# Second half of the DeltaNet's q ahead of the LRU's gate, and four square roots in one activation

## The chip, the cores and the metric

The kernel runs on one core of a Trainium2 chip. The metric is device microseconds (us) for one execution. A core has five engines with an instruction stream each: TensorE (PE, matmuls; PEld is its weight load), VectorE (DVE), ScalarE (ACT), GpSimd (POOL) and SyncE (SP, which issues most DMAs). Each engine works through its stream in the order that was written when the kernel was built, and waits on semaphores for the others.

## The reference

One layer of a hybrid diffusion backbone, for 512 latent tokens and 128 context tokens with the same weights. A normalised and modulated input goes through one wide projection `w_in`; its columns feed four mixers, each run forward and backward; their outputs go through `w_out`, then a SwiGLU feed-forward block, then a last norm. Two mixers matter here, cut to the steps that do:

```python
# RG-LRU (each direction): x = dwconv(u_x), gate = gelu(u_gate)
r, i = sigmoid(x @ w_r + b_r), sigmoid(x @ w_i + b_i)
a = exp(-8 * r * softplus(-lambda))
h = scan(a, sqrt(1 - a * a) * i * x)          # h_t = a_t h_{t-1} + b_t
out = (h_forward + h_backward) * gate

# gated DeltaNet (each direction, chunks of tokens)
q, k, v = split(silu(dwconv(u_qkv)))
A = strict_tril((k beta) k^T * decay)         # needs k
attn = tril(q k^T * decay)                    # needs q and k
u, w = solve(I + A, [v beta, k beta exp(g)])
```

## The kernel before, in words

**Staging.** Everything is fp32, with projections as three products of a high and a low part. The 640 tokens are five tiles of 128 (t = 0 to 3 latent, 4 context). The run has four parts: norms and the first projections (to about 65 us), the rest of the input projections with the mixers' first steps (65 to 350), the scans, Hyena's transforms and the output projection (350 to 580), and the feed-forward block (580 to the end).

**A projection** (`inproj`, line 490 for its load, 504 for its matmuls) makes 128 columns of `w_in` for all tokens. It loads 512 KB into one of four `raw` buffers on SP; ACT casts the high part (line 166, tile `h_g` for a DeltaNet column block, `h_lg` for a gate of the LRU, `h_s` for the SSD), DVE makes the low part (line 162); both go into two slots each (tags `hi` and `lo`). Then come 48 matmuls, 24 for each half of 320 tokens, each half in one of three PSUM banks (tag `ip`). `conv_` (lines 530 to 542) copies both halves from PSUM into one of two pads (`xpad`, lines 534 to 536), multiplies by the first tap on ACT (539) and adds the other taps on DVE (542); `conv_silu` adds a tanh on ACT (526) and a product on DVE (527).

**The DeltaNet.** `g_q(0)` and `g_q(1)` project the two halves of q into `qT[0]` and `qT[1]`; g_q(1) is called at line 989. `EN(t)` (line 999) makes, for each tile and direction, the decay matrix (`gd`, matmuls at 738 and 739, exponential on ACT at 740 into one of three `Eh` buffers), the products k k^T and k q^T (`pkk`, lines 1013 and 1014, which read both halves of q), and on DVE (line 162) the products `Nm` and `Eh`; the latter is stored to `at_d` by a DMA of POOL (1019). One of the `Eh` buffers is later the place of `xsT[0]`, which `ssd_in(0)` writes. With all of `Nm` there, the inverse begins at line 1075: `A1` is cleared (1084) and filled by copies (1078 is their helper), transposed into `Lm` (1091, 1092), inverted in 15 steps on DVE, and merged to larger blocks (`g_merge`, lines 1135 to 1199, tiles `pg`, `pu`, `b0m`, `b1m`). `A1` and its neighbours take the memory that the LRU gives back at line 1059 (`la.close()`).

**The LRU.** For i = 0, 1 and both directions: `lru_m(i)` (line 909) has gate matmuls (917), tanh on ACT (918, 920) and a product on DVE (921). `lru_x2(i)`, named `lru_f0` and `lru_f1` in the list of priorities, has an exponential and a square on ACT (940, 941) and a product on DVE (942). `lru_q` takes the square root of that product (949), `lru_e(i)` multiplies, scans (960) and combines. `lru_g(i)` projects the gate, `lru_h(i)` makes its gelu.

**What sets the order.** No order is written out by hand. Each step names itself with `PR("name")`, which looks up a number in `PRI` (lines 36 and 37): among what is ready on an engine, a planner that simulates the time when the kernel is built takes the smaller number first. Loads of weights have 11144 taken off (`HPW`), convolutions 466 (`HPC`). Numbers that matter: `g_q0` 2384, `g_q1` 5036, `lru_g0` 2433, `lru_g1` 2240, `lru_m1` 2421, `lru_f0` 1412, `lru_f1` 3633, `lru_q` 2553, `lru_e0` 1709, `lru_e1` 2530, and for `EN` `g_N0` to `g_N4` (163 to 705) and `g_A0` to `g_A4` (334 to 2820).

**Tiles of the LRU.** Two tiles `ar0` and `ar1` of [128, 7, 642] hold seven slots each (lines 876, 877); `slot(i, 4)` and `slot(i, 5)` are the inputs and results of the square roots.

Of the kernel before, what the change touches and what calls it, by code (L numbers as in the profile page):

```python
# [10 lines left out]
F32 = mybir.dt.float32  # L11
F32R = mybir.dt.float32r
AF = mybir.ActivationFunctionType
# [5 lines left out]
P = 128  # L19
# [10 lines left out]
CW = 642  # L30
# [5 lines left out]
PRI = {'start': -944, 'mod00': 2696, 'hyk11': 1265, 'mod0b': 2465, 'ln1': 1628, 'mod01': 2955, 'ln1a': 167, 'mod02': -718, 'ln1b': 103, 'pcb': 223, 'ln1c': 1485, 'hyk10': 417, 'psj': 1862, 'zs0': 2044, 'zm0': -455, 'zs1': 881, 'zm1': 8, 'zs2': -414, 'zm2': 393, 'ze': 1399, 'dt': 933, 'g_k0': 2123, 'g_k1': 2629, 'g_kch': 972, 'lru_x0': 1527, 'hyk1b': 1451, 'lru_x1': 1575, 'hyk20': 544, 'hyk21': 1740, 'hyk22': 1814, 'hyk23': 1707, 'hyk24': 1990, 'g_kc2': 276, 'g_q0': 2384, 'lru_m': 2899, 'lru_k': 1498, 'g_q1': 5036, 'lru_m0': 406, 'lru_m1': 2421, 'g_0': 4095, 'g_N1': 163, 'g_A1': 1465, 'lru_g0': 2433, 'lru_f1': 3633, 'lru_g1': 2240, 'g_N3': 705, 'g_A3': 334, 'lru_f0': 1412, 'g_N2': 541, 'g_A2': 635, 'g_v0': 548, 'g_v1': 2397, 'g_N0': 172, 'g_A0': 2820, 'lru_h0': 2965, 'lru_h1': 2619, 'g_N4': 593, 'g_A4': 618, 'ssd_i0': 2774, 'lru_q': 2553, 'lru_e0': 1709, 'ssd_i1': 2822, 'lru_e1': 2530, 'g_vt': 1745, 'lru_s': 2094, 'g_nq': 2189, 'ssd_i3': 2918, 'ssd_i2': 2870, 'gz1': 3762, 'hy_v0': 1937, 'gz0': 2627, 'hy_10': 4373, 'mod20': 2831, 'g_base': -389, 'hy_v1': 2055, 'hy_11': 2440, 'mod21': 1302, 'g_mg': 2913, 'hy_00': 2567, 'mod22': 2350, 'hy_01': 2595, 'mod23': 1837, 'g_m4': 1148, 'g_m03': 1303, 'g_m12': 2034, 'g_scan': 3264, 'ssd_0': 3102, 'g_u40': 2369, 'g_u41': 2320, 'g_u00': 1882, 'g_u01': 2336, 'g_u30': 557, 'g_u31': 2358, 'g_u10': 2369, 'g_u11': 2380, 'g_u20': 1806, 'g_u21': 2402, 'g_s40': 4492, 'g_s41': 2958, 'mod40': 2376, 'ssd_p4': 5380, 'mod41': 2698, 'g_s00': 601, 'g_s31': 2981, 'ssd_p0': 3161, 'g_s10': 2343, 'g_s21': 2586, 'mod42': 2634, 'g_o4': 2441, 'g_f4': 2509, 'ssd_p3': 3197, 'mod30': 1471, 'ssd_p1': 3326, 'g_s20': 2566, 'g_s11': 3455, 'mod43': 307, 'g_o1': 2401, 'g_f1': 1956, 'g_s30': 2992, 'ssd_p2': 2893, 'g_s01': 3006, 'g_o3': -46, 'g_f3': 2760, 'mod31': 4255, 'ssd_e': 4063, 'g_o2': 2169, 'g_f2': 883, 'g_o0': 697, 'g_f0': 1847, 'po_lru': 2438, 'po_lru1': 2582, 'mod32': 2201, 'mod33': 1666, 'po_lru0': 1699, 'po_gdn': 5099, 'po_gdn1': 5500, 'mod50': 2718, 'po_gdn0': 4149, 'po_ssd': 3645, 'mod51': 556, 'po_ssd1': 4259, 'po_ssd0': 4824, 'hy_c': 4288, 'hy_t': 3649, 'hy_f4': 2554, 'mod52': 89, 'hy_f3': 2521, 'hy_f1': 2545, 'hy_f2': 2488, 'hy_f0': 2124, 'hy_y1': 664, 'hy_y0': 4124, 'gam': 412, 'po_x4': 1254, 'po_x1': 4228, 'po_x2': 4233, 'po_x0': 3441, 'po_x3': 3747, 'po_s': 2293, 'out04': 482, 'out01': 2542, 'out02': 9821, 'out00': 8067, 'out03': 6014, 'out14': 2981, 'out11': 4232, 'out12': 6019, 'out10': 3671, 'out13': 5720, 'ln2': 3582, 'mod53': -782, 'ffn': 2467}  # L36
PRI.update({'g_scan': 2100, 'g_u40': 2200, 'g_u41': 2220, 'g_u20': 2240, 'g_u21': 2260, 'g_u30': 2280, 'g_u31': 2300, 'g_u10': 2320, 'g_u11': 2340, 'g_u00': 2360, 'g_u01': 2380, 'g_s40': 2400, 'g_s41': 2420, 'g_s00': 2440, 'g_s31': 2460, 'g_s10': 2480, 'g_s21': 2500, 'g_s20': 2520, 'g_s11': 2540, 'g_s30': 2560, 'g_s01': 2580, 'hy_c': 1000, 'hy_t': 2600, 'g_o4': 2660, 'g_f4': 2720, 'hy_f0': 2780, 'hy_f1': 2840, 'hy_f2': 2900, 'g_o1': 2960, 'g_f1': 3020, 'hy_f3': 3080, 'g_o2': 3140, 'g_f2': 3200, 'hy_f4': 3260, 'hy_y0': 3320, 'g_o0': 3380, 'g_f0': 3440, 'hy_y1': 3500, 'g_o3': 3560, 'g_f3': 3620, 'mod40': 2700, 'mod41': 2850, 'mod42': 3000, 'mod43': 4200, 'gam': 3000, 'ln2': 4955, 'ffn': 6500, 'ln2b': 5080, 'ffn0': 5050, 'ssd_0': 3000, 'ssd_p4': 3700, 'po_lru': 2500, 'po_hy': 3690, 'po_lru0': 3720, 'ssd_p0': 3780, 'ssd_p1': 3830, 'ssd_p2': 3880, 'ssd_p3': 3930, 'po_lru1': 3980, 'ssd_e': 4040, 'ssd_m0': 4070, 'ssd_y0': 4100, 'po_hy0': 4130, 'po_gdn': 4190, 'ssd_m1': 4210, 'ssd_y1': 4240, 'po_hy1': 4270, 'mod30': 3780, 'po_gdn0': 4350, 'ssd_m2': 4410, 'ssd_y2': 4440, 'po_gdn1': 4470, 'ssd_f0': 4530, 'po_x0': 4540, 'out0': 4550, 'mod31': 3830, 'mod32': 4070, 'mod33': 4080, 'ssd_m3': 4610, 'ssd_y3': 4640, 'ssd_f1': 4670, 'po_x1': 4680, 'out1': 4690, 'h20': 4720, 'ssd_m4': 4740, 'ssd_y4': 4770, 'mod50': 4949, 'ssd_f2': 4820, 'po_x2': 4830, 'out2': 4840, 'h21': 4870, 'ssd_f3': 4900, 'po_x3': 4910, 'out3': 4920, 'h22': 4950, 'ssd_f4': 4970, 'po_x4': 4980, 'out4': 4990, 'h23': 5020, 'h24': 5040, 'mod51': 5019, 'mod53': 5039, 'po_ssd': 4000, 'po_s': 4000, 'po_w': 4470, 'ffn_w': 4845, 'ffn_s': 5080})
RG = {'pkv': 1, 'psz': 1, 'px': 1, 'pso': 1, 'pst': 1, 'p0': 1, 'sd': 1, 'pcb': 1, 'pce': 1, 'py': 1}
PRLOG = []

ROWS = {}
# [101 lines left out]
def body(nc, tc, I, O, dbg=()):  # L143
    ctx = ExitStack()
    with ctx:
        _body(ctx, nc, tc, I, O, dbg)


def _body(ctx, nc, tc, I, O, dbg):
    V, S, G, PE, SY = nc.vector, nc.scalar, nc.gpsimd, nc.tensor, nc.sync  # L150

    def PR(name):
        if name in PRI:
            tc.cur_priority = PRI[name]
        PRLOG.append((name, tc.cur_priority))

# [26 lines left out]
    def ring(k, dflt):  # L183
        return (psi, ps)[RG.get(k, dflt)]

# [687 lines left out]
    lp = la.enter_context(tc.tile_pool(name="lp", bufs=1, side="right"))  # L873


    ar = [lp.tile([P, 7, CW], F32, name=f"ar{i}") for i in range(2)]
    slot = lambda i, k: ar[i][:, k]
    bd = [pool.tile([P, 2, 2, P], F32, tag=tg, name=f"bd{tg}") for pool, tg in ((qkp, "kT1"), (mixp, "xsT1"))]
    PR("lru_m")
    for gi, nm in enumerate(("lru_w_r", "lru_w_i")):  # L880
# [62 lines left out]

    def lru_q():
        PR("lru_q")
        for i in range(2):
            for d in range(2):
                u = slot(i, 4 + d)
                S.activation(u, u, AF.Sqrt, scale=0.25)

    def lru_e(i):
        PR(f"lru_e{i}")
# [75 lines left out]
    g_v(1)  # L1028
    EN(1)
    lru_q()  # L1030
    lru_e(0)
    EN(0)
# [838 lines left out]
    for q in range(FT // 2):  # L1871
# [4 lines left out]
        u = acp.tile([P, NTOK], F32, tag="u", bufs=1, name=f"u{q}")  # L1876
# [140 lines left out]
```

## Time and profile before

| what | value |
|---|---|
| median of 3 runs | 1005.34 us (1001.15 to 1012.11) |
| the profiled execution's own time | 1005.17 us |
| its span, first to last instruction | 1003.4 us |
| mean granted clock of TensorE in the span | 0.965 |

The rows that follow the change are from the profiled execution. Times in them are microseconds from the start of the span, unless marked ns. A row of a timeline is: start, duration, engine, line, operation, what it writes and reads, how many instructions it merges, and in brackets the idle time ahead of it and what ended that. A row of instruction groups has busy time and mean duration in ns, then the idle time in front of the group. TensorE's clock has two levels, 1.2 and 2.4 GHz; the profile gives the mean granted share of the higher one.

### The profile page before, as it was taken

The numbers are of one execution on the slowest core, as the hardware profiler recorded it, in microseconds if no ns is written. First come the engines' busy times: TensorE is split into PE (matmuls) and PEld (weight loads), VectorE is DVE, ScalarE is ACT, GpSimd is POOL, SyncE is SP. The second block draws the span as 40 slices with busy tenths as digits, with TensorE's granted clock in tenths as the row PEclk, the third lists the DMA queues.
The fourth block names the chain that finished last, engine by engine and source line by source line (L and its number), as shares of the span: only waits on it lengthen the run. The fifth ranks groups of instructions, "written<-read, shape, count | busy, mean of one in ns | idle before, by whom it ended". The sixth has DMA issues, their size and how long they took to land.

```text
span 1003.4 us, 17283 instructions
## 1 busy us (share of the span) xinstructions
PE 949.8 (95%) x6837; PEld 820.8 (82%) x6837; DVE 649.5 (65%) x1162; ACT 443.2 (44%) x827; POOL 254.7 (25%) x262
## 2 busy tenths in 40 slices
PE   5999999999989999989998699999999999999995
PEld 2788887989868877866666599999999998888884
DVE  3667756869840257456799998777777777414115
ACT  3585287565565441134236454444444446122112
POOL 3115400221110120000354665444444420002001
PEclk9999996999987999999999799999999999999998
DMA  9983510432320654444234233222223336312202
GB/s 316 298 247 81 171 43 21 129 108 65 107 75 3 203 171 122 142 157 143 62 108 158 85 106 84 85 85 85 85 84 86 87 91 215 92 62 98 71 21 105
DMA packets 100654, 114.29 MB, mean 114 GB/s; under 512 B 13493, under 2 KB 77370, under 8 KB 100573
## 3 DMA queue, kind: packets, MB, share of 16 engines
q1 hardware_dynamic: 94748, 103.56, 33.7%
q0 software_dynamic: 5824, 9.63, 3.2%
q8 instruction: 54, 0.88, 0.4%
q14 instruction: 28, 0.22, 0.1%
HBM read 100.39 MB, written 12.24 MB: 112 GB/s over the span
## 4 chain that ended last, share of the span: by engine, by line
PE 78%; DVE 8%; ACT 6%; DMA 3%; issue 3%; POOL 2%; SPq 0%; POOLq 0%; ACTq 0%; DVEq 0%
PE dn L1959 15%; PE ip_g L504 4%; PE ip_h L504 3%; PE pm L358 3%; PE ip_s L504 2%; PE pplru L1581 2%; PE pphy L1581 1%; PE ip_hv L504 1%; PE pzz L589 1%; PE hpy L1398 1%; PE pab L1374 1%; PE pv L1234 1%; PE ip_gz L504 1%; PE ip_lg L504 1%; DVE x2a L162 1%
## 5 line engine op out<-in xcount | busy, mean ns | idle before, releaser
L1959 PE MATMUL dn<-h_d,alo 128*128 128x512 f32 x220 | 86.4, 393 | 0.2 <-DVE alo L162 0.2
L1959 PE MATMUL dn<-l_d,ahi 128*128 128x512 f32 x220 | 86.4, 397 | 0.0
L1959 PE MATMUL dn<-h_d,ahi 128*128 128x512 f32 x220 | 85.1, 393 | 0.6 <-DVE u L162 0.5
L162 DVE TENSOR_TENSOR l_d<-r_d,h_d 128x1024 fp32r<-128x1024 f32 x22 | 27.0, 1226 | 77.9 <-ACT h_d L166 76.6
L166 ACT CAST h_d<-r_d 128x1024 fp32r<-128x1024 f32 x22 | 23.1, 1048 | 93.9 <-PE dn L1959 82.7
L1959 PEld LDWEIGHTS dn<-h_d,alo 128*128 128x128 f32 x220 | 41.4, 188 | 10.6 <-DVE alo L162 0.5
L1959 PEld LDWEIGHTS dn<-h_d,ahi 128*128 128x128 f32 x220 | 41.2, 188 | 10.5 <-DVE u L162 0.9
L1959 PEld LDWEIGHTS dn<-l_d,ahi 128*128 128x128 f32 x220 | 41.3, 188 | 9.0
L358 PE MATMUL pm<-wm,sc 128*32 128x256 f32 (+1 forms) x320 | 33.8, 472 | 2.8 <-ACT sc L291 2.8
L1992 POOL TENSOR_TENSOR x<-x,aux 128x512 f32<-128x512 f32 x5 | 7.3, 1462 | 96.2 <-ACT aux L1989 96.2
L264 POOL TENSOR_TENSOR ss<-ss,mh 128x1 f32<-128x1 f32 (+1 forms) x11 | 8.0, 727 | 89.0 <-DVE ss L1945 71.7
L731 POOL DMA_DIRECT2D RT<-grd x20 | 11.1, 559 | 73.4 <-PE pce L1528 44.2
L1826 POOL TENSOR_TENSOR sms<-r_u,sms 128x512 f32<-128x512 f32 x11 | 14.9, 1352 | 45.7 <-DVE op_g4S L162 4.5
L264 POOL TENSOR_TENSOR ro<-ro,mh 128x4 f32<-128x4 f32 x5 | 5.4, 1089 | 74.2 <-DVE ro L267 74.2
L1826 POOL TENSOR_TENSOR sms<-r_g,sms 128x512 f32<-128x512 f32 x11 | 14.7, 1334 | 35.8 <-DVE op_u5S L162 4.3
L360 ACT COPY mr<-pm 128x256 f32<-128x256 f32 (+1 forms) x20 | 8.3, 413 | 29.9 <-PE pm L358 27.7
L162 DVE TENSOR_TENSOR l_h<-r_h,h_h 128x1024 fp32r<-128x1024 f32 x4 | 4.8, 1212 | 25.3 <-ACT h_h L166 17.9
L1822 POOL TENSOR_TENSOR sms<-sms,r_u 128x512 f32<-128x512 f32 x11 | 16.6, 1506 | 11.0 <-DVE op_g0S L162 4.7
L162 DVE TENSOR_TENSOR alo<-act,ahi 128x640 fp32r<-128x640 f32 x22 | 18.1, 824 | 1.4
L528 POOL MEMSET xpad<- 128x2 f32 x10 | 1.0, 100 | 69.8 <-DVE kT L527 22.9
L1820 POOL TENSOR_TENSOR sms<-r_u,r_u 128x512 f32<-128x512 f32 x11 | 14.4, 1311 | 16.7 <-DVE tmp L162 2.5
L358 PEld LDWEIGHTS pm<-wm,sc 128*32 128x32 f32 x320 | 9.8, 113 | 10.8 <-issue 3.8
(1294 smaller groups left out, 2949.0 us busy)
## 6 DMA issues: line engine op xcount, KB each, us to landing
wm<-w_mod SPq DMA_DIRECT2D x48, 512.0 KB, 4.9
r_g<-w_gate SPq DMA_DIRECT2D x22, 512.0 KB, 3.8
r_u<-w_up SPq DMA_DIRECT2D x22, 512.0 KB, 5.1
r_d<-w_down SPq DMA_DIRECT2D x22, 512.0 KB, 3.9
cs<-k_cs POOLq DMA_DIRECT2D x8, 512.0 KB, 6.0
r_g<-w_in SPq DMA_DIRECT2D x6, 512.0 KB, 6.6
xs_dram<-xt SPq DMA_DIRECT2D x5, 512.0 KB
at_d<-Eh POOLq DMA_DIRECT2D x10, 256.0 KB, 2.4
```

What stands on the lines that cost most here:

```text
L162: V.tensor_tensor(out, a, b, op=op)
L166: S.copy(hi, src)
L264: last_pow[0] = G.tensor_tensor(ap, ap, m.to_broadcast(list(ap.shape)), op=ALU.pow)
L358: last_mm[0] = PE.matmul(pm[j * 32:j * 32 + 32, :w], sc2[:, kt, :], wms[kt // nk][:, kt % nk, :], start=(kt < 4), stop=(kt >= 4))
L504: PE.matmul(pj[:, :320], a[:, kt, :], b[:, kt, c], start=(n == 0), stop=(n == 23))
L589: PE.matmul(pzz[t][:, :280], hx[:, k0 + k, t * P:(t + 1) * P], w[:, k, :], start=(q == 0 and n == 0), stop=(q == 2 and n == 3 * nk - 1))
L731: G.dma_start(RT[32 * d + 8:32 * d + 10, b], grd[m * 8 + d * 4:m * 8 + d * 4 + 4, :, t].rearrange("h a c -> a h c"))
L1581: PE.matmul(po, a[:, i, tk], b[:, i], start=(n == 0), stop=(n == last))
L1820: G.tensor_tensor(sf("S1"), A[1, 0], A[1, 1], op=ALU.add)
L1822: G.tensor_tensor(sf("S2"), sf("S1"), A[0, 0], op=ALU.subtract)
L1826: G.tensor_tensor(sf("S4"), A[0, 1], sf("S2"), op=ALU.subtract)
L1959: PE.matmul(po[t], a[f][:, tk], b[:, i, :], start=(f == 0 and pi == 0), stop=(f == FT - 1 and pi == 2))
```

## The change

The step `g_q1` gets the number 2390 in place of 5036, so it comes right behind `g_q0`. The two tiles of the LRU become one tile `ar` of five slots for each i and one tile `au` of the two slots that the square roots use; the slots' places change and their sum stays at 14. `lru_q` takes the square root of all of `au`, 2568 columns, with one activation in place of four of 642.

```diff
 RG = {'pkv': 1, 'psz': 1, 'px': 1, 'pso': 1, 'pst': 1, 'p0': 1, 'sd': 1, 'pcb': 1, 'pce': 1, 'py': 1}
+PRI.update({'g_q1': 2390})
 PRLOG = []
...
-    ar = [lp.tile([P, 7, CW], F32, name=f"ar{i}") for i in range(2)]
-    slot = lambda i, k: ar[i][:, k]
+    ar = lp.tile([P, 2, 5, CW], F32, name="ar")
+    au = lp.tile([P, 2, 2, CW], F32, name="au")
+    slot = lambda i, k: au[:, i, k - 4] if k in (4, 5) else ar[:, i, min(k, 4)]
...
     def lru_q():
         PR("lru_q")
-        for i in range(2):
-            for d in range(2):
-                u = slot(i, 4 + d)
-                S.activation(u, u, AF.Sqrt, scale=0.25)
+        S.activation(au, au, AF.Sqrt, scale=0.25)
```

## Rows read from the trace of the kernel before

**Rows 1.** The page: busy time of the engines, and granted clock in 40 slices.
```profile
PE 949.8 (95%) x6837; PEld 820.8 (82%) x6837; DVE 649.5 (65%) x1162; ACT 443.2 (44%) x827; POOL 254.7 (25%) x262
...
PEclk9999996999987999999999799999999999999998
```

**Rows 2.** PE by stretches: stretch, length, busy (instructions), granted clock, DMA share, GB/s.
```profile
140.00:180.00 40.00, 38.10 (x188) 0.79 0.15 40
180.00:230.00 50.00, 49.79 (x330) 1.00 0.31 99
230.00:240.00 10.00, 8.14 (x45) 0.83 0.20 59
240.00:280.00 40.00, 40.00 (x410) 1.00 0.41 118
280.00:330.00 50.00, 44.50 (x1029) 0.76 0.12 37
330.00:420.00 90.00, 89.89 (x804) 1.00 0.52 155
```

**Rows 3.** Waits of PE, 100 to 350: total us, times, longest.
```profile
PE pu L1198 <- ACT b1m L1194: 2.6, 1, 2.6
PE ip_s L504 <- ACT xpad L534: 2.1, 1, 2.1
PE gd L738 <- ACT ar L918: 1.9, 1, 1.9
```

**Rows 4.** Timeline of PE, 130 to 188.
```profile
131.20 1.58 PE L504 MATMUL ip_g<-hhi,h_g 128*128 128x320 f32 x8
...
150.33 0.90 PE L504 MATMUL ip_g<-hhi,h_g 128*128 128x320 f32 x5
153.12 0.49 PE L738 MATMUL gd<-RT,LT 10*128 10x512 f32 x1 [1.90 <-ACT ar L918]
...
159.45 2.33 PE L504 MATMUL ip_lg<-hhi,h_lg 128*128 128x320 f32 x8
...
173.71 1.34 PE L504 MATMUL ip_g<-hhi,l_g 128*128 128x320 f32 x8
...
187.44 0.71 PE L1014 MATMUL pkk<-qT,knT 64*128 64x128 f32 x8
```

**Rows 5.** Groups of ACT's instructions, 125 to 185.
```profile
L949 ACT ACT_TABLE_LOAD x4 | 5.1, 1283 | 0.1
...
L949 ACT ACTIVATE ar<-ar 128x642 f32<-128x642 f32 x4 | 3.0, 741 | 0.0
...
L166 ACT CAST h_lg<-r_lg 128x1024 fp32r<-128x1024 f32 x2 | 2.1, 1046 | 5.3 <-PE ip_g L504 5.3
...
L918 ACT ACT_TABLE_LOAD x1 | 1.3, 1283 | 0.0
```

**Rows 6.** Timeline of SP's queue: loads of q's weights.
```profile
63.92 2.55 SPq L490 DMA_DIRECT2D r_g<-w_in  x2
```

**Rows 7.** Groups of DVE's instructions, 185 to 225.
```profile
L162 DVE TENSOR_TENSOR Eh<-pkk,Eh 128x256 f32<-128x256 f32 x20 | 8.0, 419 | 0.1
L162 DVE TENSOR_TENSOR Nm<-pkk,Eh 128x256 f32<-128x256 f32 x20 | 7.9, 417 | 6.3 <-PE pkk L1014 5.5 <-ACT Eh L740 0.8
```

**Rows 8.** Groups of DVE's instructions, 125 to 185.
```profile
L960 DVE TENSOR_TENSOR_SCAN ar<-ar,colv 128x512 f32<-128x512 f32 x4 | 5.1, 1279 | 0.1
L162 DVE TENSOR_TENSOR ar<-ar 128x642 f32<-128x642 f32 x6 | 4.9, 825 | 10.4 <-ACT ar L949 10.4
...
L960 DVE TENSOR_TENSOR_SCAN ar<-ar 128x128 f32<-128x128 f32 x4 | 1.6, 399 | 0.0
```

**Rows 9.** The chain that ended last, 209 to 233: start, us, what.
```profile
214.78 2.76 DMA at_d<-Eh
...
225.51 2.11 DVE Lm L1092
```

**Rows 10.** Timeline of POOL: the clear of the inverse's first tile.
```profile
182.31 0.74 POOL L1084 MEMSET A<- 128x768 f32 x1 [14.43 <-ACT gt L967]
```

## The prediction

> **What bounds the kernel now.** I began with the busy shares and the slices of the granted clock: TensorE (PE) is busy 95% of the span, and its clock drops in a few slices only [rows 1]. So the end is set by PE's own work plus what PE loses: idle time, and time at the lower of its two clock levels. Then I took PE stretch by stretch [rows 2]. Lost time is the length less busy, plus length times (1 - granted clock):
> - A, 140 to 180: 1.9 idle and 0.21 x 40 = 8.4 of clock, 10.3 together.
> - B, 230 to 240: 1.9 idle and 0.17 x 10 = 1.7 of clock, 3.6.
> - C, 280 to 330: 5.5 idle and 0.24 x 50 = 12.0 of clock, 17.5.
> From 180 to 230, 240 to 280 and 330 to 420 there is next to nothing (0.2, 0 and 0.1).
>
> Next the waits of PE [rows 3]: A's idle time is one wait of 1.9 for an LRU activation, B's is one of 2.1 for the copy of a projection to its pad, C's longest is 2.6 in the merges of the DeltaNet's inverse. Then the timeline of PE [rows 4]. The q projection `g_q(1)` is 48 matmuls in two halves. Its first half runs at 131.2. Its second half is strewn: a few matmuls at 150.33, some between, the last eight from 173.71. In the middle PE waits 1.9 and then runs at the lower level, 1.2 GHz instead of 2.4: eight matmuls of the LRU's gate take 2.33 at 159.45, eight of the same shape 1.34 at 173.71. The first product that needs all of q runs at 187.44, though `EN(2)`, which wants it, had its decay matmul on PE at 153.12. So q's second half holds three things for some 40 us: one of three projection banks, one of two weight slots (hi, lo), one of two pads; and behind it `EN` holds PSUM banks and its three `Eh` buffers.
>
> **The change part by part.**
>
> *Square roots.* Today four activations of 128x642 at 0.741, and between them other functions, so that ScalarE (ACT) loads a table eight times: four loads for the roots at 1.283, four back (L918, L920, L740, L930) [rows 5]. After: one activation of 128x2568, one load, one load back. Loads saved: 6 x 1.283 = 7.7. The one root is not in the trace: not under 0.74 (one of today's), not over 4 x 0.741 = 2.96. Two rows of one input, 642 columns at 0.741 and a cast of 1024 at 1.046, give 0.80 ns a column, so 0.74 + 1926 x 0.0008 = 2.28; I take 2.3. ACT gains 7.7 + 0.7 = 8.4 in all. How much of it reaches the end? PE waited for ACT once here, 1.9 [rows 3]. Ahead of that wait stand two roots and four loads, 2 x 0.74 + 4 x 1.28 = 6.6; q's own convolution comes in ahead instead, two passes and two copies, some 2.2 (an estimate, three of the 0.74). The net 4.4 covers the 1.9. So that wait goes; what is late next is `EN`, whose products need VectorE (DVE).
>
> ACT's four loads for the roots have 0.1 of idle time in front of them, all told [rows 5]. The Trainium skill, in "ScalarE: Activation LUTs", section "What ACT_TABLE_LOAD costs", prices a switch at 1283 ns of load and some 1380 ns of drain, 2.66 us. The load agrees to the nanosecond; of the drain no row here shows anything. By that page ACT would be 16 us ahead, I would leave no stall over in A below, and the sum would be 988.6 where by the rows it is 990.7.
>
> *q's second half earlier.* The priority falls from 5036 to 2390, behind `g_q0` at 2384 and ahead of `lru_g0` at 2433 (smaller goes first). PE work: none added, 24 matmuls x 0.147 (1.34 less the overlap, per eight) = 3.5 move ahead of the gate. Its weights' load stands on SP at 63.92 with the one before it [rows 6], 67 ahead of its use, right behind `g_q0`'s as the program has it, though at 5036 its number was the higher by far; a lower number can bring it forward by the 2.6 of both issues at most, and the loads behind it wait no longer than that, all with more than that in hand: 0. The gate starts 3.5 later, which its readers, the LRU's last products on DVE, must bear.
>
> In return the bank, the slot and the pad come free at about 142 instead of 175, and q is whole at about 148: 141 for the matmuls, then the pad, the taps and the gate of the convolution. `EN` can run from there instead of from 187. Its DVE part is 20 + 20 operations at 0.418, 16.7 [rows 7]. In its new place DVE has the LRU: ten microseconds of today's idle time there are waits for the roots themselves [rows 8]. I take `EN` as done by 175 to 190; today its last store goes out at 214.78 and the inverse's transposes follow at 225.51 [rows 9].
>
> *What that is worth to PE.*
> - A: 10.3 lost, bounds 0 to 10.3 for what returns. With a whole slot pair, gate, v and `EN` can feed PE without a break. I leave one stall of the size of B's, 2.1, since `EN`'s small matmuls now alternate with DVE here: 8.2 back.
> - B: 0 to 3.6. `ssd_in(0)` writes into the buffer of `Eh` and waits for its last store [rows 9]; with `EN` done before, the copies flow. I take 3.6.
> - C: the merges wait on ACT, DVE and GpSimd, and none of their own steps gets shorter. What changes is that they begin earlier against PE's reserve of projections (hv, gz, h). Bounds: all that PE gained before is given back here (-11.8), to all returned (+17.5). I take half of the idle time, 2.7, and nothing of the clock.
> Sum: 8.2 + 3.6 + 2.7 = 14.5. The profiled execution took 1005.17 (span 1003.4 and 1.8 around it), 0.17 under the median of the three runs, so I use one for the other: 1005.2 - 14.5 = 990.7, rounded to 991.
>
> *What the single root costs.* It needs all four of its inputs, so the first scan, today behind the first of four roots, waits for the last. All four scan groups then come behind it: two scans of 1.28 and 0.40 and a product of 0.82 each [rows 8], 2.5 x 4 = 10 in a row where now one group is left after the last root: 7.5 later. The LRU's memory is needed by the inverse's first clear, at 182.31 [rows 10], whose data come only after 214.78. So 30 of slack cover the 7.5, even if `EN` (16.7) goes first on DVE: 24. I count 0; without cover it would be 24 - 7.7 = 16 at worst on the inverse's start.
>
> **The rivals.**
> 1. *Given back at the merges.* The inverse starts no earlier because its memory, not `EN`, comes last: `lru_f1` has the low rank 3633, and with `EN` now ahead on DVE its last input to the root is late. PE gains A and B (11.8), arrives early at the merges and waits there. Two thirds given back, 8: 1005.2 - 11.8 + 8 = 1001. For it: all other steps of the LRU and of `EN` outrank `lru_f1`. Against: 30 us of slack. Chance 0.20.
> 2. *The whole of C goes too.* With 20 us of lead the merges hide under projections: another 14.8 of C at most; I take 14: 991 - 14 = 977. For it: from 240 to 280 projections kept PE full, at a clock of 1.00, beside the inverse [rows 2]. Against: PE runs in a written order, and the merges' matmuls stand in it between the projections. Chance 0.13.
> 3. *Slower: the root stands waiting at the head of ACT.* If it is issued before its last input is made, all behind it wait: the exponentials of `EN` and the copies that empty PE's banks. Three banks hold 3 x 3.5 = 10.6 of projection work, so it decides from a wait of 10.6 on; `EN`'s 16.7 on DVE [rows 7] ahead of the last input would give 16.7 - 10.6 = 6.2 of stall, and a stretch at the lower clock such as A's after 1.9 of idle time, 8.4. A's own loss stays, since `EN` is held up too; B goes: 1005.2 + 6.2 + 8.4 - 3.6 = 1016. Against: `EN`'s products need exponentials from the same ACT, so DVE soon runs out of them and takes the LRU's operation. The Trainium skill, in "TensorE: Matmul & The Clock Gate", section "Architectural detail: the array is 16x 32x32, not 1x 128x128", calls ScalarE's queue strict FIFO, which is the rule that this needs; no row here shows ACT passing one by. Chance 0.15.
> That the change doesn't do what it says, q's second half staying behind the gate because the planner orders by its own clock, is part of rival 1's time: only A's 1.9 and some of the clock, about 1000.
>
> **How the numbers follow.** Forecast 991: chance 0.52, own range 983 to 998. Rivals 0.20, 0.13 and 0.15. Range 8 in 10: 977 to 1010, which leaves out half of rival 2 and nearly all of rival 3, 0.2. The runs before spread over 1%, so 1% (10) is about what can be told from no change. Faster by over that (under 995): 0.44 of the forecast's 0.52 and all of rival 2, 0.57. Slower (over 1015): 0.13, most of rival 3. Within: the other 0.08 of the forecast, rival 1 and the rest of rival 3, 0.30.
>
> **What would show it.** Right: L949 once with one load; the 48 matmuls of q's half in one run ending at about 141; the products of `EN` at 150 to 190; no wait of PE for L918; granted clock near 1.00 over 140 to 180; no wait of `ip_s` for the pad; the transposes near 205. Wrong: PE's idle time in 150 to 200 above 3 with waits for ACT; the merges' idle time above 6; the inverse's clear after 205. What is most open is the planner's order, which the diff doesn't show.

## The result, and the profile after

| | before | after |
|---|---|---|
| median on the same chip | 1006.49 us (4 runs, 1001.15 to 1012.11) | 988.89 us (4 runs, 987.34 to 993.70) |
| ratio, 95% interval | 1 | 0.9859 (0.9820 to 0.9898) |
| the profiled execution's own time, span | 1005.17, 1003.4 | 990.24, 988.5 |
| mean granted clock | 0.965 | 0.973 |

The change saves 1.4%, and the forecast of 991 is 2 off. The steps behind it fared less evenly than their sum. Lines of the kernel after differ by one from those before: the root is L948, the tanh of q L527, the copies into the inverse's first tile L1077. Four executions further down (two of same_table_q, one each of fill_pool and pad_first) took over 1.5% more than the fastest of their kernel; ratios and medians leave them out.

The page of the kernel after, busy time and granted clock, as [rows 1]:

```profile
PE 935.1 (95%) x6837; PEld 809.4 (82%) x6837; DVE 642.7 (65%) x1162; ACT 435.2 (44%) x818; POOL 257.4 (26%) x262
...
PEclk9999999989979999999999799999999999999998
```

Two readings. ACT is 8.0 us shorter (8.4 forecast). And PE's idle time, span less busy, is what it was: 1003.4 - 949.8 = 53.6 before, 988.5 - 935.1 = 53.4 after. What came back is clock: 1003.4 x 0.035 = 35.1 at the lower level's price before, 988.5 x 0.027 = 26.7 after. The other 6 of the 14.9 lie inside PE's busy time at its granted clock, and these views don't break them down.

PE by stretches in the kernel after, columns as in [rows 2]; the last row is a stretch that the prediction did not use:

```profile
140.00:180.00 40.00, 40.00 (x246) 1.00 0.23 62
180.00:230.00 50.00, 47.06 (x302) 0.93 0.33 102
230.00:240.00 10.00, 10.00 (x70) 1.00 0.24 63
240.00:280.00 40.00, 37.50 (x675) 0.96 0.39 114
280.00:330.00 50.00, 46.99 (x880) 0.90 0.16 48
330.00:420.00 90.00, 88.64 (x733) 0.96 0.53 158
420.00:480.00 60.00, 58.10 (x341) 1.00 0.44 143
```

The kernel before had this in the last one, and this as PE's longest wait there:

```profile
420.00:480.00 60.00, 54.75 (x337) 0.97 0.48 154
```

```profile
PE pplru L1581 <- ACT h_olru L166: 3.6, 1, 3.6
```

With the prediction's measure, idle plus length times (1 - clock), before against after: A 10.3 to 0; 180 to 240 3.8 to 6.4; 240 to 330, where the merges are in both, 17.5 to 12.1; 330 to 420 0.1 to 5.0; 420 to 480 7.0 to 1.9. So +10.3, -2.6, +5.4, -4.9, +5.1.

The waits of PE, 100 to 350, as [rows 3]:

```profile
PE pu L1179 <- ACT b0m L1174: 2.4, 1, 2.4
PE pu L1197 <- ACT b1m L1193: 2.1, 1, 2.1
PE pls L1063 <- ACT v_tm L1053: 1.7, 1, 1.7
PE ip_s L505 <- ACT xpad L537: 1.3, 1, 1.3
```

A's wait for the LRU's tanh is gone. B's single wait of 2.1 has become two of 1.7 and 1.3, at 213.00 and 215.72.

ACT's timeline around the one root, columns as in [rows 4]:

```profile
152.00 0.73 ACT L527 ACTIVATE xpad<-qT 128x642 f32<-128x642 f32 x1
153.50 0.60 ACT L741 ACTIVATE Eh<-gd 128x512 f32<-128x512 f32 x1 [0.77 <-PE gd L740]
154.11 1.28 ACT L948 ACT_TABLE_LOAD   x1
155.41 2.35 ACT L948 ACTIVATE au<-au 128x2568 f32<-128x2568 f32 x1
157.78 1.28 ACT L527 ACT_TABLE_LOAD   x1
159.07 0.74 ACT L527 ACTIVATE xpad<-qT 128x642 f32<-128x642 f32 x1
```

One load there and one back as written in the diff, a root of 2.35 where 2.28 was estimated. But the first load stands ahead of q's second tanh, which waits 154.11 to 159.07. DVE in the same stretch:

```profile
157.79 3.04 DVE L163 TENSOR_TENSOR ar<-ar,au 128x642 f32<-128x642 f32 x4 [3.30 <-ACT au L948]
160.75 0.82 DVE L528 SCALAR_TENSOR_TENSOR qT<-xpad,qT 128x642 f32<-128x642 f32 x1
...
167.26 0.40 DVE L959 TENSOR_TENSOR_SCAN au<-ar 128x128 f32<-128x128 f32 x1
...
169.28 0.74 DVE L163 TENSOR_TENSOR Nm<-pkk,Eh 128x256 f32<-128x256 f32 x2
```

q is whole at 161.6, not 148, and four products and eight scans run ahead of `EN`'s first. The clear and the transposes of the inverse ([rows 9, 10]):

```profile
193.92 0.74 POOL L1083 MEMSET A<- 128x768 f32 x1 [3.98 <-ACT gt L966]
...
L1090 DVE STREAM_TRANSPOSE Lm<-A x1: 1246/1246/1246, 208.0 to 208.0; 128x1024 f32<-128x1024 f32 x1
L1091 DVE STREAM_TRANSPOSE Lm<-A x1: 2037/2037/2037, 212.6 to 212.6; 128x1024 f32<-128x1024 f32 x1
```

The second transpose starts 12.9 earlier than the 225.51 of before, the first 9.4 earlier (217.4 before); 20 was the forecast for both.

### The profile page after: what moved, and what is told of

It is laid out like the page before. It is cut to its first block, busy times and chain, and to the rows that moved or that the text cites. A ratio compares the mean times of both kernels' runs of the same rounds, so it can differ in the third digit from the quotient of the medians.

```text
span 988.5 us, 17280 instructions
## 1 busy us (share of the span) xinstructions
PE 935.1 (95%) x6837; PEld 809.4 (82%) x6837; DVE 642.7 (65%) x1162; ACT 435.2 (44%) x818; POOL 257.4 (26%) x262
## 4 chain that ended last, share of the span: by engine, by line
PE 82%; DVE 6%; ACT 4%; DMA 3%; issue 2%; POOL 1%; SPq 0%; POOLq 0%; DVEq 0%; ACTq 0%
PE dn L1958 15%; PE ip_g L505 4%; PE ip_h L505 3%; PE pm L359 3%; PE ip_s L505 2%; PE ip_gz L505 2%; PE ip_lg L505 2%; PE pphy L1580 2%; PE pplru L1580 1%; PE ip_hv L505 1%; PE hpy L1397 1%; PE pzz L590 1%; PE pab L1373 1%; DMA dskip<-ssd_d 1%; PE po L1281 1%
## 5 line engine op out<-in xcount | busy, mean ns | idle before, releaser
L1958 PE MATMUL dn<-l_d,ahi 128*128 128x512 f32 x220 | 86.3, 397 | 0.0
L1958 PEld LDWEIGHTS dn<-h_d,ahi 128*128 128x128 f32 x220 | 41.2, 188 | 10.5 <-DVE u L163 0.9
L359 PE MATMUL pm<-wm,sc 128*32 128x256 f32 (+1 forms) x320 | 30.0, 473 | 2.8 <-ACT sc L292 2.8
L1991 POOL TENSOR_TENSOR x<-x,aux 128x512 f32<-128x512 f32 x5 | 7.3, 1466 | 96.2 <-ACT aux L1988 96.2
L1819 POOL TENSOR_TENSOR sms<-r_g,r_g 128x512 f32<-128x512 f32 x11 | 19.7, 1791 | 19.2 <-DMA r_g<-w_gate 5.0
L505 PE MATMUL ip_g<-hhi,l_g 128*128 128x320 f32 x96 | 20.4, 329 | 0.0
L505 PE MATMUL ip_g<-hlo,h_g 128*128 128x320 f32 x96 | 19.1, 319 | 0.0
L163 DVE TENSOR_TENSOR alo<-act,ahi 128x640 fp32r<-128x640 f32 x22 | 18.1, 824 | 1.4
L505 PE MATMUL ip_g<-hhi,h_g 128*128 128x320 f32 x96 | 18.0, 313 | 1.1 <-ACT zt L595 1.1
```

Source lines behind the costliest of these rows:

```text
L163: V.tensor_tensor(out, a, b, op=op)
L359: last_mm[0] = PE.matmul(pm[j * 32:j * 32 + 32, :w], sc2[:, kt, :], wms[kt // nk][:, kt % nk, :], start=(kt < 4), stop=(kt >= 4))
L505: PE.matmul(pj[:, :320], a[:, kt, :], b[:, kt, c], start=(n == 0), stop=(n == 23))
L1819: G.tensor_tensor(sf("S1"), A[1, 0], A[1, 1], op=ALU.add)
L1958: PE.matmul(po[t], a[f][:, tk], b[:, i, :], start=(f == 0 and pi == 0), stop=(f == FT - 1 and pi == 2))
```

## The experiments

Executions differ by up to 4 us in the part before 126, which no edit touches. So the table counts from PE's first matmul of the LRU's gates (`lpg`, 126.7 before, 126.6 after): to the start of the second transpose into `Lm`, and to the last matmul of the DeltaNet's output projection (`ppgdn`, 511.7 before, 494.9 after). "Lost" is idle and clock together. The ratio is to the kernel before on the same chip.

| kernel | q's half | roots | ratio (95%) | lost 140-180 | lost 210-240 | to `Lm` | to `ppgdn` |
|---|---|---|---|---|---|---|---|
| before | late | four, strewn | 1 | 10.3 | 3.9 | 98.8 | 385.0 |
| same_table | late | strewn, no loads | 0.9969 (0.9941-0.9998) | 0 | 2.1 | 89.4 | 377.2 |
| q_only | early | strewn | 0.9969 (0.9943-0.9996) | 5.2 | 2.4 | 90.3 | 378.1 |
| same_table_q | early | strewn, no loads | 0.9963 (0.9933-0.9993) | 0 | 2.4 | 85.7 | 373.7 |
| root_only | late | joined | 0.9920 (0.9889-0.9951) | 0 | 10.6 | 96.2 | 373.6 |
| roots_row_late_q | late | three and one | 1.0045 (1.0012-1.0077) | 0 | 12.4 | 96.0 | 386.2 |
| roots_in_a_row | early | three and one | 0.9901 (0.9864-0.9938) | 0 | 3.8 | 85.5 | 369.4 |
| after | early | joined | 0.9859 (0.9820-0.9898) | 0 | 6.2 | 86.0 | 368.3 |
| after_again | early | joined | 0.9855 (0.9812-0.9899) | 0 | 5.1 | 85.9 | 365.4 |
| root_behind_q | early | joined, behind q | 0.9836 (0.9807-0.9864) | 0 | 1.1 | 86.8 | 361.4 |
| root_behind_q2 | early | the same again | 0.9818 (0.9776-0.9861) | 0 | 1.4 | 87.1 | 364.3 |
| fill_pool | early | joined | 0.9918 (0.9883-0.9953) | 0 | 2.9 | 86.3 | 370.0 |
| fill_split | early | joined | 0.9925 (0.9899-0.9950) | 0 | 4.7 | 86.3 | 369.1 |
| pad_first | early | joined | 1.0039 (1.0006-1.0072) | 0 | 5.7 | 89.0 | 381.1 |

One warning for the whole table: the planner orders everything anew behind any edit. Only in same_table and same_table_q is the written order of all five engines that of its partner (before, and q_only), loads apart. In the others the merges and what follows stand in another order too.

### The loads alone: same_table

```diff
-                S.activation(u, u, AF.Sqrt, scale=0.25)
+                S.activation(u, u, AF.Square, scale=0.25)
```

> The kernel before with a square in place of each of the four roots, so the DeltaNet and the transforms get the same numbers and the LRU others. A square needs no other table than tanh and exp: the written order of all five engines stays what it was, and nothing goes but eight loads, 10.3 of ACT. Theory (A's loss came of the loads): 140 to 180 loses under 2 in place of 10.3; as q stays late, the inverse's transposes come at most 4 earlier, half or more of the gain is given back by 240, and the time is 0 to 6 under that of the kernel before. Rival 1 (A's loss came of q's bank, slot and pad): 140 to 180 still loses over 6, no difference in time. Rival 2 (the loads alone are the whole of the change): 10 or more under the kernel before.

PE by stretches, A and the merges:

```profile
140.00:180.00 40.00, 40.00 (x249) 1.00 0.21 54
...
280.00:330.00 50.00, 45.36 (x835) 0.73 0.16 49
```

Measured: 999.70 against 1001.09. With nothing gone but eight loads, and q as late in PE's order as before, A's whole 10.3 returns, the clock's 8.4 with the stall's 1.9. The SSD's first matmul comes 9.5 earlier (counted as in the table: 182.3 - 128.7 against 189.8 - 126.7). The merges lose 4.6 + 13.5 = 18.1, as much as before, so of the 10.3 some 7.8 is left at `ppgdn` and 3 by the ratio. The theory had A and the time right. Two of its steps were wrong: the second transpose comes 9.4 earlier, not 4 at most, and nothing is given back by 240 (180 to 240 loses 2.1, before 3.8). Rival 2 falls, for the loads are not the whole change. Rival 1 falls as the sole cause: A does not need q's bank, slot and pad to come free. That q's place can shorten A's loss too is seen in the next kernel.

### q's half alone, and without the loads: q_only, same_table_q

q_only has the line `PRI.update({'g_q1': 2390})` and nothing else of the change.

> Only the number of g_q1 is changed (5036 to 2390); the four square roots stay apart, in the two tiles of before. Theory (both parts feed the same stretch: q's second half held a bank, a weight slot and a pad, and the table loads held up ACT): the q matmuls come in one run, but ACT keeps its eight loads (10.3 us), so q is whole some 5 us later than in the changed kernel and a short wait of PE for ACT stays; 140 to 180 loses 3 to 5 instead of 10.3; about 995 us. Rival 1 (q's place alone does it): as the changed kernel, about 989. Rival 2 (the table loads alone do it): no change, about 1005.

same_table_q adds the edit of same_table to it.

> The kernel with only q's half moved, and a square in place of each of the four roots (the LRU gets other numbers): its order stays, eight loads of a table go, nothing is joined. Theory (what the change needs is that the loads are gone and q is early; the joining is only the means): 140 to 180 loses under 2 of the 5.2 there, time 986 to 992, as the changed kernel. Rival (the joined root also changes the order of the LRU's scans and EN on DVE, and that carries part): 993 to 998, next to the kernel with q alone.

Measured: 998.04 against 1000.95, and 997.62 against 1001.09. q's half alone makes the inverse 8.5 earlier and leaves half of A's loss; by the ratio it is worth 0.3%, not the 1% of its theory. Its stall is nearly as long as that of 1.90 before:

```profile
PE pkk L1014 <- ACT ar L919: 1.6, 1, 1.6
```

The stretch at the lower clock behind it is much shorter, with PE busy all the time in both. Before, and then q_only:

```profile
154.00:170.00 16.00, 16.00 (x54) 0.50 0.13 34
170.00:172.00 2.00, 2.00 (x12) 0.72 0.00 0
```

```profile
150.00:156.00 6.00, 6.00 (x19) 0.50 0.34 91
156.00:158.00 2.00, 2.00 (x9) 0.81 0.00 0
```

That is some 17 us at 1.2 GHz before and some 7 in q_only, so the length of a stall does not give the price of the clock behind it. Why it is shorter here was not tested.

Without the loads A is clean and the second transpose as early as in the kernel after. Its profiled execution is 4.4 ahead of q_only's at `ppgdn`, but the ratio moves by 0.06% only, so the theory of same_table_q, 986 to 992, was wrong. The time lies in its rival's range, though the cause read from the traces is another than the rival's order of scans and `EN`. An early q and no loads at all are together worth 0.4%; the other 1.0% of the change's 1.4% comes with the joined root and the order that the planner finds around it (four roots close together, unjoined, reach 0.9901 below). Where the time stays is seen in q_only, in the last two matmuls of the LRU's gate projection and in the inverse's clear:

```profile
195.23 0.46 PE L505 MATMUL ip_lg<-hhi,l_lg 128*128 128x320 f32 x2
```

```profile
207.70 0.74 POOL L1085 MEMSET A<- 128x768 f32 x1 [3.78 <-ACT gt L968]
```

and in a wait of PE that neither before nor after has:

```profile
PE pg L1151 <- DVE b0m L1148: 4.5, 3, 4.0
```

In the kernel after, the last five `ip_lg` start at 173.22. Here two of its matmuls are left standing behind `EN`'s products; the gate's gelu, the LRU's last products and with them its memory come late, the clear is at 207.70 instead of 193.92, and the first transpose starts 88.3 from the first `lpg`, in the kernel after 81.4. PE then stands at the merges; 240 to 280 loses 10.4 in q_only and 11.2 in same_table_q, 4.1 in the kernel after. This is rival 1 of the prediction (the LRU's memory comes last), by the gate's projection instead of by `lru_f1`. It is read from the traces; no run moved these two matmuls alone.

### The roots alone: root_only, roots_row_late_q, roots_in_a_row

root_only has the new tiles and the one activation, with g_q1 at 5036.

> Only the square roots are joined (one activation of 2568 columns, the tiles ar and au); g_q1 keeps 5036. Theory (both parts): the wait of 1.9 for an LRU activation goes and with it some of the half clock, but EN still has no q until 180; 140 to 180 loses 4 to 7; about 1000 us. Rival 1 (q's place alone): about 1005. Rival 2 (the table loads alone): about 989.

PE by stretches:

```profile
140.00:180.00 40.00, 40.00 (x246) 1.00 0.18 46
180.00:210.00 30.00, 30.00 (x179) 0.89 0.34 107
210.00:240.00 30.00, 26.26 (x138) 0.77 0.21 67
```

Measured: 993.60 against 1000.95. A, where the theory still had 4 to 7, is clean with q as late as ever (`EN`'s products run to 213 on PE and to 223 on DVE), in line with same_table. 180 to 240 pays for it with 13.9: the inverse is only 2.6 earlier, and PE waits 3.7 for the pad of the SSD.

The next two have four roots on the new tiles, issued behind the last square. roots_row_late_q has g_q1 at 5036 as well.

```diff
-        S.activation(au, au, AF.Sqrt, scale=0.25)
+        with tc.issue_after(last_ex[0].ins):
+            for i in range(2):
+                for d in range(2):
+                    u = slot(i, 4 + d)
+                    S.activation(u, u, AF.Sqrt, scale=0.25)
```

> The same four roots, three and one, with q's second half at its old priority: the kernel before but for the place of the roots. Theory 1 (A's loss came of the eight loads that stood among the LRU's tanhs ahead of the gate's matmuls, and of nothing else): 140 to 180 loses under 2 of its 10.3, the inverse stays as late as in the kernel with the joined root alone (last store of EN near 223), 180 to 240 loses 8 or more, time 993 to 998. Rival (A's loss came of q's late bank, slot and pad): 140 to 180 loses 6 to 10, time 999 to 1005.

> The changed kernel with four roots of 642 columns, issued behind the last square; in ACT's order three stand together ahead of q's second tanh and the fourth behind it, so four loads of a table in place of two. Theory 1 (what counts is that the roots stand together and not strewn among the tanhs, the joining itself buys only loads): 140 to 180 loses under 2, q is whole 2.6 to 4 us later than in the changed kernel, and the time is 988 to 993. Theory 2 (each load of a table on ACT's chain is paid in full by the end): the two more loads, 2.6, and the wider sum of the four roots, 0.7, come out at 3 or more, 992 to 997. Rival (the joined root costs by making all scans wait, and single roots let the scans start early): under 987.

Measured: 1008.43 and 991.87 against 1003.51. The late one wins A (10.3) and is slower than the kernel before, by 0.45%. PE arrives early at the SSD's projections, and waits there:

```profile
PE ip_s L505 <- ACT xpad L535: 5.8, 1, 5.8
```

The theory had A right and the end wrong (993 to 998). The early one is where theory 1 put it (988 to 993), two or three above the changed kernel (991.87 against the 989.58 of after_again). The intervals overlap; as far as they tell, the joining buys about its two loads, 2.6, and little else. q is whole 1.5 later than in the kernel after, counted as in the table, where 2.6 to 4 was expected. What q's place is worth depends on the order that it meets: 16.6 us between these two kernels, which differ in the one priority, 0.6% with the joined root, 0.3% with the roots strewn.

### The root behind q's tanh: root_behind_q, twice

```diff
-        S.activation(au, au, AF.Sqrt, scale=0.25)
+        with tc.issue_after(q_tanh.ins):
+            S.activation(au, au, AF.Sqrt, scale=0.25)
```

> The changed kernel, with the one root issued on ACT behind the tanh of q's second half (in the changed kernel that tanh stands behind the root and its two table loads, and q is whole at 161.6 where 148 was expected). Theory (the root in front of the tanh is what made EN late): q whole at about 157, EN's first products on DVE ahead of the LRU's scans at about 158 instead of 169, its last store 5 us earlier, and the end 2 to 4 us earlier: 985 to 987. Rival (the inverse's start waits for the LRU's memory, cleared at 193.92, not for EN): the clear is no earlier or later, and the time stays at 989 to 991.

> The changed kernel with the joined root issued behind q's second tanh, once more in more rounds. If what it gained is real: ratio to the kernel before 0.981 to 0.986. If it was the luck of four executions: 0.986 to 0.990.

ACT and DVE of the first run:

```profile
153.64 0.73 ACT L528 ACTIVATE xpad<-qT 128x642 f32<-128x642 f32 x1
154.39 1.28 ACT L950 ACT_TABLE_LOAD   x1
155.69 2.35 ACT L950 ACTIVATE au<-au 128x2568 f32<-128x2568 f32 x1
157.94 0.72 ACT L617 ACTIVATE pnq<-qT 128x642 f32<-128x642 f32 x1
```

```profile
162.23 0.40 DVE L961 TENSOR_TENSOR_SCAN au<-ar 128x128 f32<-128x128 f32 x1
162.55 0.40 DVE L163 TENSOR_TENSOR Nm<-pkk,Eh 128x256 f32<-128x256 f32 x1
```

Measured: 983.96 against 1000.95 and 983.85 against 1001.09, the best of all. q is whole at 155.2, the root starts 0.3 later than in the kernel after, and `EN`'s first product comes at 162.55, between the scans. The times were those of the theory or better, but not by its way: what that gives is not an earlier inverse (86.8 and 87.1 against 86.0), and `EN`'s last store goes out at 210.79, in the kernel after at 207.92. The stretch that differs is 210 to 240: the two runs of copies into the inverse's tile lie apart on ACT (201.63 and 208.93), with a pad's copy at 206.83 between them, and 1.1 and 1.4 are lost where the kernel after loses 6.2 and 5.1. The second run gives that back in the merges: 240 to 330 loses 20.7, in after_again 15.6. The intervals of its ratio and of the kernel after overlap, so the 0.2 to 0.4% between them is likely, not settled.

### The copies into the inverse's tile: fill_pool, fill_split, pad_first, beside after_again

In the kernel after ACT has two runs of three such copies, with one activation between them, and then what PE waits for in 210 to 240:

```profile
203.76 4.13 ACT L1077 COPY A<-Nm 32x640 f32<-32x640 f32 x3
207.91 0.74 ACT L616 ACTIVATE pnq<-qT 128x642 f32<-128x642 f32 x1
208.56 3.98 ACT L1077 COPY A<-Nm 32x640 f32<-32x640 f32 x3
212.57 0.65 ACT L1053 COPY v_tm<-pkv 128x256 f32<-128x256 f32 x2
...
215.39 0.27 ACT L537 COPY xpad<-ip_s 128x128 f32<-128x128 f32 x1
```

The step `g_base` has the number -389, below the value's copies and the pad's, so 8.1 us of copies go first. fill_pool gives two of the eight to GpSimd:

```diff
-        (S.copy, V.tensor_copy, S.copy, S.copy)[k % 4](dst, src)
+        (S.copy, V.tensor_copy, G.tensor_copy, S.copy)[k % 4](dst, src)
```

> The changed kernel, with two of the eight copies that fill the inverse's first tile on GpSimd instead of ACT. Theory (PE's waits at 211 to 218 in the changed kernel, 1.7 and 1.3 and 3.5 of clock behind them, come from ACT doing 8.1 us of these copies in one go ahead of the copies that empty PE's banks): ACT has 2.7 us less there, the two waits shrink to under 1.5 together; 985 to 987 us. Rival (GpSimd's copies are slower than ACT's 1.37 each, the inverse's transposes come later, and what is won at 211 is lost at the merges): 989 to 992.

Measured: 994.85 against 1000.95, above both ranges. GpSimd's copies took 1.34 and 1.38, no longer than ACT's. But PE's two waits are 0.5 and 2.5, the same 3.0 together, where the theory had under 1.5. 210 to 240 loses 2.9, half, and what went is the clock's part; 280 to 330 loses 3.9 + 11.0 = 14.9 where the kernel after loses 8.0 and, run again, 10.0. What was won ahead of the merges was lost in them.

fill_split orders the copies by direction and gives those of the second the number 2000.

> The changed kernel with the eight copies into the inverse's first tile in another order: first the four of one direction, then the four of the other at a lower rank, so that ACT can take the value's transposes and the pad's copies between them. Theory (the loss in 210 to 240 comes of some 8 us of such copies in one run on ACT): that loss falls from 6.2 to under 3, the second transpose into Lm ends up to 4 us later, and the time is 983 to 988 if the merges do not take it back, 988 to 991 if they do. Rival (the loss there comes of PE's own order, or of DVE): 210 to 240 still loses 5 or more, 988 to 992.

Measured: 995.54 against 1003.51. It is no test of its theory: the planner put five of ACT's six copies ahead of the value's first copy all the same (203.70 to 211.10), and 210 to 240 loses 4.7.

pad_first issues three of ACT's six behind the pad's copies of the second SSD block.

```diff
+    pad_cp = cps[-1]
...
+            with (tc.issue_after(pad_cp.ins) if d and q != 1 else ExitStack()):
```

> The changed kernel with three of ACT's six copies into the inverse's first tile issued behind the pad's copies of the second SSD block, for which PE waited. Theory (the loss in 210 to 240 comes of 8 us of such copies in a row on ACT): the wait for the pad and the one for the value's copy go, 210 to 240 loses under 2.5 in place of 5 to 6, the second transpose into Lm ends 2 to 4 later, time 984 to 990. Rival (PE would wait for something else there): 210 to 240 loses 4 or more, no gain, 988 to 994.

ACT of this kernel, and PE's waits from 210 to 300:

```profile
210.97 0.33 ACT L537 COPY xpad<-ip_s 128x192 f32<-128x192 f32 x1
211.17 0.29 ACT L538 COPY xpad<-ip_s 128x128 f32<-128x128 f32 x1
211.33 4.20 ACT L1079 COPY A<-Nm 32x640 f32<-32x640 f32 x3
```

```profile
PE ip_gz L505 <- ACT xpad L536: 3.4, 1, 3.4
...
PE ip_s L505 <- ACT xpad L536: 1.5, 1, 1.5
```

Measured: 1005.16 against 1001.09. The two waits at 213 and 215.7 are gone, so they were the copies' doing, as the theory says. The second transpose is 3.0 later, as expected. But PE waits 1.5 and 3.4 for the next pads instead, 210 to 240 loses 5.7, and the time is 0.4% above the kernel before, so the theory's loss and time were wrong. The rival has the mechanism, PE waiting for something else, and not the time. 12.8 are gone by `ppgdn`; which part of that is the later inverse and which the planner's new order of the merges was not separated.

The kernel after itself, on the chip of fill_split and of the roots in a row:

> The changed kernel once more, beside the three others of this chip. Both theories: 987 to 991 where the kernel before takes 1001 to 1006; 140 to 180 without loss of PE, and some 6 us lost in 210 to 240.

Measured: 989.58 against 1003.51, as expected.

## Why the prediction was right, and which of its steps were not

- **A, 8.2 back.** Measured 10.3. Size near, cause half right. The prediction gave ACT the stall's 1.9 (a net 4.4 ahead of the tanh) and gave the clock's 8.4 to q's bank, slot and pad coming free. same_table has q as late as ever in PE's order and A at 0: the 8.4 was the wake of the 1.9, and both go with the loads. q's early place, with the loads still there, gives back half (q_only, 5.2 lost), so that part was not wrong but not needed. "I leave one stall of the size of B's, 2.1" was caution without need.
- **The drain.** The two loads of the kernel after run without a gap to speak of: 154.11 + 1.283 = 155.39, and the root starts at 155.41. The eight loads that same_table drops take 443.2 - 432.7 = 10.5 off ACT's busy time. The Trainium skill, in "ScalarE: Activation LUTs", section "What ACT_TABLE_LOAD costs", has another 1380 ns of drain to each switch. The SSD's first matmul came 9.5 earlier in same_table, which the loads alone account for; by that page eight switches would be 21 (an estimate, eight times 2.66), and no row here shows the half beyond the loads.
- **B, 3.6 back.** Wrong: 2.6 more were lost, one stall later. "With `EN` done before, the copies flow" failed twice. `EN` ran from 169 to 207, not to 175 or 190: q was whole late, and its 16.7 of DVE took 38 among convolutions, casts and the LRU's products. And the inverse's copies came to stand where `EN` had stood, 8.1 us on ACT ahead of the pad's; pad_first shows that those copies made the two waits. The forecast "no wait of `ip_s` for the pad" came out false, and so did three other marks: q's 48 matmuls in one run by 141, `EN` at 150 to 190, the transposes near 205 (208.0 and 212.6). None of the signs of being wrong appeared. The prediction also misread one row: 214.78 is the ninth of `EN`'s ten stores before; the last goes out at 222.03, in the kernel after at 207.92.
- **q whole at about 148.** Wrong by 13. The 48 matmuls were done at 145, strewn among the LRU's, not in one run by 141; and the root with its two loads came ahead of the second tanh on ACT. That is rival 3's place, the root at the head of ACT, with q behind it in place of PE's banks; PE lost nothing there, and putting the root behind the tanh (root_behind_q) made q whole at 155.2.
- **C, 2.7 back, "nothing of the clock".** The size was too small and the split the wrong way round: in 240 to 330 5.4 came back, all of it clock (12.0 to 6.6), while idle time stayed 5.5. What followed was not foreseen at all: 4.9 lost in 330 to 420, 5.1 back in 420 to 480, where the wait of `pplru` for a cast of ACT, 3.6, is no more.
- **The joined root's scans cost 0.** Held. The clear came at 193.92, 11.6 later than before, and the second transpose 12.9 earlier. Cover was there.
- **The rivals.** Rival 1's mechanism is real and was avoided: it is what q_only does, at a wait of 4.5 in the merges. The kernel of the change escapes it because its order has the gate's projection done at 174. That this follows from joining the roots is seen in the orders, not derived: the planner's choice remains the open part, as the prediction said. Rival 2 would have needed all of C.

So the sum, 14.5 against 14.9, was right by two errors that met, which is luck as far as the closeness goes: A and C gave 4.8 more than forecast, B 6.2 less, and 0.2 net came from 330 to 480. Those stretches sum to 13.3, but by 330 the two kernels are not at the same work. Counted by the work, as in the table, 16.7 came back up to the last `ppgdn` (385.0 to 368.3) and 1.9 were lost behind it, where PE's idle time grew from 24.5 to 27.6. Of the 16.7, 3.1 is idle time (14.8 to 11.7), about 8 is clock, and some 5 lies in busy time that no view resolved.

## What to carry to other kernels

When a short stall of the bottleneck engine is followed by its lower clock, price the two together, and look for what causes the stall alone: here 1.9 us of it carried 8.4, and 1.6 us in q_only 3.6. A stretch that is made clean can be worth little until the next wait downstream moves too: A came back in ten kernels here, and the time went from 1.8% less to 0.45% more, according to when the next consumers (pads, the inverse, the merges) were ready. Where a planner orders the work, test a cost by an edit that leaves the written order alone, such as another function of the same table, before believing edits that change it.

## What the runs showed of the hardware that was not expected

- A stall of PE of 1.90 us was followed by some 17 us at 1.2 GHz, one of 1.60 us in q_only by some 7, with PE busy 100% in both stretches.
- The granted clock's share of the loss was the part that moved: idle time 53.6 and 53.4, clock 35.1 and 26.7.
- The square root of 2568 columns took 2.352 us, one of 642 0.741: 0.836 ns for each added column, against the 0.80 of the estimate. Four in one cost 0.61 less than four by themselves.
- A copy of 640 columns on 32 partitions, with its rearranged pattern, took ACT 4.13 / 3 = 1.38 us, more than an activation of 642 columns on 128 partitions at 0.74.
